# Block-diagonal 128x128 tiles for the inverted chunk matrices of a delta-rule recurrence

## The chip, the core and the metric

The kernel runs on one core of a Trainium2 chip. The metric is the device time of one execution in microseconds. Each time shown is the median of several executions. One further execution is recorded by the hardware profiler, and the rows below come from that one.

Names of engines: PE is the matrix engine, and PEld its loading of weights, which can run beside the products. DVE is the vector engine, ACT the scalar engine, POOL the third elementwise engine, and SP issues most of the DMAs.

## What is computed

One layer of a hybrid decoder over 1024 tokens of width 1024, in float32. A normalised input goes through one combined projection, then through two branches: sliding-window attention and an RWKV-7 recurrence with 8 heads of size 64. The branches are gated and merged, and a squared-ReLU MLP follows. The recurrence is what matters here:

```python
def step(S, inp):
    r_t, w_t, k_t, v_t, a_t, b_t = inp
    sa = jnp.einsum('bhij,bhj->bhi', S, a_t)
    S = S * w_t[:, :, None, :] + sa[..., None] * b_t[:, :, None, :] + v_t[..., None] * k_t[:, :, None, :]
    return S, jnp.einsum('bhij,bhj->bhi', S, r_t)
```

## The kernel before

**The recurrence in chunks.** The 1024 steps are cut into 16 chunks of 64 tokens. Heads go in pairs, so that a pair fills 128 partitions. A unit is one pair over one half of the sequence, that is 8 chunks. There are 8 units, run one after the other. For each unit `unit_e` prepares decays, keys and receptances. `unit_m` inverts a 64x64 triangular matrix for each chunk and head. `unit_c` carries the state from chunk to chunk.

**Where the inverses lie.** `unit_m` leaves the inverses, transposed, in the tile XT of shape 128x8x64. Even chunks of the unit stand on partitions 0 to 63 and odd chunks on 64 to 127. The middle index counts chunk pair and head. The inverse is finished by two ACT copies of 32x256 elements (line 619).

**The chain of one chunk** (`unit_c`) has these steps, each of which needs the one before it:

1. `ry` (line 636, PE): the old state times keys and receptances, one 128x128 product.
2. `G` (line 638, DVE): adds half of `ry` to the right-hand side `Rs`, a slice of the tile G0.
3. `pu` (lines 641 to 642, issued at line 162, PE): the inverse times `Rs`, one 64x64 product for each of two heads.
4. `UV` (line 643, DVE): copies `pu` out.
5. `pd` (line 646, PE): the update of the state, one 128x128 product.
6. `sbd` (lines 653 and 656, DVE): two operations that write the new state, which the next `ry` needs.

The weights of a float32 product are loaded twice and its columns run twice, so each of `ry` and `pd` has 2 PE rows in the trace, and `pu`, with its two heads, has 4.

**The order of work.** A scheduler lays down one fixed order for each engine when the kernel is built. The recurrence has a raised priority. Between its steps the scheduler puts "fill": products of the projections and gates (`ps_m`, line 156, 128x128 weights and 512 columns), attention (`ps_t`, `pt_t`, `po`) and low-rank projections (`ps_l`). A list of steps, PLAN, says which fill is on offer beside which unit. After the last unit the rest of the fill runs, then the branch projections, the output projection and the MLP. PE runs its rows strictly in the order laid down.

**Shapes of the array.** A PE row of the trace shows which part of the array a product uses: 128\*128 is all of it, 64\*64 a quarter, and 64\*128, 128\*64 and 32\*32 occur as well. The fill is 128\*128 almost everywhere. `pu` is 64\*64, and so are `ps_g`, `ps_z` and `ps_x` of `unit_m`. The readout `py` at the end of a unit is 128\*64.

Of the kernel before, what the change touches and what calls it, by code (L numbers as in the profile page):

```python
# [11 lines left out]
F32 = mybir.dt.float32  # L12
# [8 lines left out]
P = 128  # L21
# [37 lines left out]
def hybrid_block(ctx, tc, x_ap, xt_ap, win_ap, lora_ap, wbr_ap, wout_ap, wff1_ap, wff2_ap, cst_ap,  # L59
                 vec_ap, eye_ap, amk_ap, out_ap, dbg=None):  # L60
    nc = tc.nc
    V, A, G, PE = nc.vector, nc.scalar, nc.gpsimd, nc.tensor
# [28 lines left out]
    def c_(name):  # L91
        o, n = COFF[name]
        return cst[0][:, o:o + n] if o < CKEEP else cst[1][:, o - CKEEP:o - CKEEP + n]
# [65 lines left out]
    def in_order(mms, after=None):  # L159
        for out, lhsT, rhs, start, stop in mms:  # L160
            with tc.issue_after(after) if after is not None else nullcontext():
                after = PE.matmul(out=out, lhsT=lhsT, rhs=rhs, start=start, stop=stop).ins  # L162
        return after
# [77 lines left out]
    def phase1():  # L241
        st = ExitStack()
        lp = st.enter_context(tc.tile_pool(name="lpool", bufs=1))
        rp = st.enter_context(tc.tile_pool(name="rpool", bufs=1))
# [203 lines left out]
                    nc.sync.dma_start(out=g_d[p][:, sl], in_=t)  # L448

        sbd = [lp.tile([P, 128], F32, name=f"sbd{i}") for i in range(2)]  # L450
        for t in sbd:
            G.memset(t, 0.0)
        ln_d = [dram.tile([64, 256], F32, name=f"ln_d{i}") for i in range(8)]
        lx_d = [dram.tile([P, 128], F32, name=f"lx_d{i}") for i in range(8)]
# [115 lines left out]
        def unit_m(p, hf, X):  # L570
            SA, UV, un = X["SA"], X["UV"], X["un"]
            G0 = rp.tile([P, 4, 128], F32, tag="G0", name="G0", bufs=1)
            half_ = [slice(0, 64), slice(64, 128)]
            ps = pp.tile([P, 4, 2, 64], F32, tag="c", name="ps_g", bufs=1)
            for i in range(4):
                for h in range(2):
                    for par in range(2):
                        uc, vc = half_[par], half_[1 - par]
                        PE.matmul(out=ps[uc, i, h], lhsT=SA[vc, par, 2 * i + h, :],
                                  rhs=UV[vc, 2 * i + par, h * 64:h * 64 + 64], start=True, stop=True)  # L580
            A.copy(out=G0, in_=ps.rearrange("p a b c -> p a (b c)"))
            XT = rp.tile([P, 8, 64], F32, tag="XT", name="XT", bufs=2)
            G.memset(XT, 0.0)
            lx = lx_d[un].rearrange("(q l b u) (c t) -> q b (u c) l t", l=8, b=2, u=2, t=16)
            for q in range(4):
                for b in range(2):
                    o = 32 * (q % 2) + 16 * b
                    s0 = 32 * q + 16 * b
                    nc.sync.dma_start(out=XT[s0:s0 + 16, :, o:o + 16], in_=lx[q, b])
            XD = rp.tile([P, 8, 64], F32, tag="DZ", name="XD", bufs=1)  # L590
            V.transpose(out=XD.rearrange("p a b -> p (a b)"), in_=XT.rearrange("p a b -> p (a b)"))
            ps = pp.tile([P, 8, 64], F32, tag="c", name="ps_z", bufs=1)
            for l in range(8):
                for par, uc in enumerate(half_):
                    PE.matmul(out=ps[uc, l], lhsT=SA[uc, par, l], rhs=XD[uc, l], start=True, stop=True)
            V.tensor_mul(out=XD, in0=ps, in1=c_("m16").unsqueeze(1).broadcast_to([P, 8, 64]))
            ps = pp.tile([P, 8, 64], F32, tag="c", name="ps_x", bufs=1)
            for l in range(8):
                for uc in half_:
                    PE.matmul(out=ps[uc, l], lhsT=XD[uc, l], rhs=XT[uc, l], start=True, stop=True)  # L600
            V.tensor_add(out=XT, in0=XT, in1=ps)
            DZ = rp.tile([P, 2, 8, 32], F32, tag="DZ", name="DZ", bufs=1)
            DT, Z = DZ[:, 0], DZ[:, 1]
            tops = [slice(64 * par, 64 * par + 32) for par in range(2)]
            lows = [slice(64 * par + 32, 64 * par + 64) for par in range(2)]
            for ta in tops:
                V.transpose(out=DT[ta], in_=XT[ta, :, 0:32])
            ps = pp.tile([P, 8, 32], F32, tag="c", name="ps_z", bufs=1)
            for l in range(8):
                for par, (ta, lb) in enumerate(zip(tops, lows)):  # L610
                    PE.matmul(out=ps[lb, l], lhsT=SA[ta, par, l, 32:64], rhs=DT[ta, l], start=True, stop=True)
            for lb in lows:
                A.copy(out=Z[lb], in_=ps[lb])
            ps = pp.tile([P, 8, 32], F32, tag="c", name="ps_x", bufs=1)
            for l in range(8):
                for ta, lb in zip(tops, lows):
                    PE.matmul(out=ps[ta, l], lhsT=Z[lb, l], rhs=XT[lb, l, 32:64], start=True, stop=True)
            for ta in tops:
                A.copy(out=XT[ta, :, 32:64], in_=ps[ta])
            X.update(G0=G0, XT=XT)  # L620

        def unit_c(p, hf, X):
            us = slice(hf * HALF, (hf + 1) * HALF)
            ARf, UV, BKt, SR, bv, wc, G0, XT = (X[n] for n in ("ARf", "UV", "BKt", "SR", "bv", "wc", "G0", "XT"))
            Yt = rp.tile([P, 4, 2, 64], F32, tag="Yt", name="Yt", bufs=2)
            for c in range(8):
                par, cp = c % 2, c // 2
                first = hf == 0 and c == 0
                uc, vc = slice(64 * par, 64 * par + 64), slice(64 - 64 * par, 128 - 64 * par)
                cur, nxt = sbd[par], sbd[1 - par]  # L630
                ry = pp.tile([P, 2, 64], F32, tag="r", name="ry", bufs=1)
                Rs = G0[:, cp, :]
                if first:
                    G.memset(Yt[vc, cp], 0.0)
                else:
                    PE.matmul(out=ry.rearrange("p a b -> p (a b)"), lhsT=ARf[:, cp, par], rhs=cur, start=True,
                              stop=True)
                    V.tensor_add(out=Rs[uc], in0=Rs[uc], in1=ry[uc].rearrange("p a b -> p (a b)"))
                    A.copy(out=Yt[vc, cp], in_=ry[vc])
                pu = pp.tile([P, 128], F32, tag="c", name="pu", bufs=1)  # L640
                last = in_order([(pu[uc, h * 64:h * 64 + 64], XT[uc, 2 * cp + h], Rs[uc, h * 64:h * 64 + 64], True,
                                  True) for h in range(2)])
                V.tensor_copy(out=UV[uc, c, :], in_=pu[uc])
                if hf == 0 or c < 7:
                    pd = pp.tile([P, 128], F32, tag="c", name="pd", bufs=1)
                    PE.matmul(out=pd, lhsT=BKt[:, c], rhs=UV[:, c], start=True, stop=True)
                    if not first:
                        sw = rp.tile([P, 128], F32, tag="sw", name="sw", bufs=2)
                        A.activation(out=sw, in_=cur, func=AF.Copy, scale=wc[:, c:c + 1])
                    for h in range(2):  # L650
                        hs = slice(h * 64, h * 64 + 64)
                        if first:
                            V.tensor_scalar(out=nxt[hs, hs], in0=pd[hs, hs], scalar1=wc[hs, c:c + 1],
                                            scalar2=None, op0=ALU.mult)
                        else:
                            V.scalar_tensor_tensor(out=nxt[hs, hs], in0=pd[hs, hs], scalar=wc[hs, c:c + 1],
                                                   in1=sw[hs, hs], op0=ALU.mult, op1=ALU.add)
# [73 lines left out]
        for n in range(8):  # L731
            p, hf = n // 2, n % 2
            with tc.high_priority(offset=HP_C):
                unit_m(p, hf, xs[n])
            if hf == 0 and p + 1 < NPAIR:
                zproj(p + 1)
            if n + 1 < 8:
                estage(n + 1)
            with tc.high_priority(offset=HP_C):
                unit_c(p, hf, xs[n])  # L740
            fill(PLAN[n + 1])
        st.close()

    def gate(i):
        w = load_w(win_ap[20 + i])
        for hf in range(2):
# [3 lines left out]
            nc.sync.dma_start(out=gate_d[i][:, hf * HALF:(hf + 1) * HALF], in_=t)  # L750

    phase1()
    bst = ExitStack()
    bp = bst.enter_context(tc.tile_pool(name="bpool", bufs=1))
    yh = [bp.tile([P, T], F32R, name=f"yh{k}") for k in range(8)]
    yl = [bp.tile([P, T], F32R, name=f"yl{k}") for k in range(8)]
    for k in range(8):
        t = bp.tile([P, T], F32, tag="yt", name="yt", bufs=3)
# [35 lines left out]
    h = [hall[:, k] for k in range(NK)]  # L794
# [404 lines left out]
```

## Time and profile before

| what | value |
|---|---|
| time, median of 3 runs | 1538.51 us (1537.07 to 1538.57) |
| profiled execution, its own time | 1539.05 us |
| its span, first to last instruction | 1537.3 us |
| mean granted TensorE clock | 0.999 |
| PE busy | 1491.2 us, 97% of the span |
| DVE busy | 1039.3 us, 68% |
| ACT busy | 638.9 us, 42% |
| POOL busy | 195.3 us, 13% |

The span leaves out 1.75 us of the execution's own time. Busy time is a sum over instructions. Products are pipelined and their recorded ends are modelled, so what one product costs is read from the distance between starts, not from its duration.

### The profile page before, as it was taken

How to read it: one execution, taken by the hardware profiler on the slowest of the kernel's cores; microseconds unless marked ns; L12 is line 12 of the kernel's file. 1: busy time of each engine (PE TensorE's matmuls, PEld its weight loads, DVE VectorE, ACT ScalarE, POOL GpSimd, SP SyncE). 2: the span in 40 equal slices, each digit the busy share in tenths (PEclk: the TensorE clock that was granted, in tenths of full speed). 3: DMA queues.
4: the chain of work that ended last, by engine and by line, in shares of the span. 5: the costliest groups of instructions: out<-in, count | busy, mean ns of one | idle time of the engine just before them, and what ended most of it. 6: DMA issues, size and time to landing. Idle time of an engine off the chain costs nothing.

```text
span 1537.3 us, 22192 instructions
## 1 busy us (share of the span) xinstructions
PE 1491.2 (97%) x8396; PEld 1179.0 (77%) x8396; DVE 1039.3 (68%) x2055; ACT 638.9 (42%) x1126; POOL 195.3 (13%) x117
## 2 busy tenths in 40 slices
PE   5999999999999999999999989999999999999998
PEld 5877767777777777788878777878787878787776
DVE  4232678888989875344656569495968587776767
ACT  6322446556545655532224343242334243424332
POOL 1000000000000000000000112322323232323230
PEclk9999999999999999999999999999999999999999
DMA  5455334334322324372442111112011111111112
GB/s 191 164 154 139 109 117 133 111 97 118 97 83 65 99 97 140 126 268 103 157 152 89 41 41 49 62 41 69 31 66 41 69 42 55 55 54 43 55 55 110
DMA packets 99771, 145.65 MB, mean 95 GB/s; under 512 B 26448, under 2 KB 48848, under 8 KB 99664
## 3 DMA queue, kind: packets, MB, share of 16 engines
q1 hardware_dynamic: 99664, 144.23, 28.6%
q8 instruction: 66, 1.08, 0.3%
q14 instruction: 41, 0.34, 0.1%
HBM read 108.54 MB, written 35.65 MB: 94 GB/s over the span
## 4 chain that ended last, share of the span: by engine, by line
PE 76%; DVE 18%; issue 2%; DMA 2%; ACT 1%; SPq 0%; DVEq 0%; ACTq 0%
PE ps_m L156 31%; PE psy L982 17%; PE psx L982 12%; DVE wlo L924 2%; PE po L156 2%; PE ps_o L915 1%; PE pu L162 1%; DVE h L1082 1%; DVE c L987 1%; DVE tlo L1010 1%; DVE c L1057 1%; DVE c L1015 1%; DVE c L1017 1%; PE pk L238 1%; PE ps_s L162 1%
## 5 line engine op out<-in xcount | busy, mean ns | idle before, releaser
L156 PE MATMUL ps_m<-uh,wlo 128*128 128x512 f32 x576 | 235.4, 409 | 0.0
L156 PE MATMUL ps_m<-ul,whi 128*128 128x512 f32 x576 | 234.3, 407 | 0.0
L156 PE MATMUL ps_m<-uh,whi 128*128 128x512 f32 x576 | 232.9, 404 | 0.0
L982 PE MATMUL psy<-T,whi 128*128 128x512 f32 x512 | 159.6, 393 | 0.0
L156 PEld LDWEIGHTS ps_m<-uh,wlo 128*128 128x128 f32 x576 | 108.6, 189 | 21.2 <-issue 0.6
L156 PEld LDWEIGHTS ps_m<-uh,whi 128*128 128x128 f32 x576 | 108.6, 189 | 21.1 <-issue 0.8
L156 PEld LDWEIGHTS ps_m<-ul,whi 128*128 128x128 f32 x576 | 108.7, 189 | 20.1 <-issue 0.7
L982 PEld LDWEIGHTS psy<-T,whi 128*128 128x128 f32 x512 | 96.1, 188 | 21.6
L982 PE MATMUL psx<-tlo,whi 128*128 128x512 f32 x256 | 101.9, 398 | 7.3 <-DVE tlo L1010 7.3
L982 PE MATMUL psy<-T,wlo 128*128 128x512 f32 x256 | 101.4, 396 | 4.4 <-DVE wlo L924 4.4
L149 DVE TENSOR_TENSOR wlo<-wraw,whi 128x512 fp32r<-128x512 f32 x101 | 67.8, 687 | 55.9 <-ACT whi L148 55.8
L924 DVE TENSOR_TENSOR wlo<-fraw,whi 128x1024 fp32r<-128x1024 f32 x47 | 62.3, 1326 | 62.8 <-ACT whi L923 62.8
L982 PE MATMUL psx<-thi,wlo 128*128 128x512 f32 x256 | 101.1, 396 | 0.9 <-DVE h L1082 0.9
L982 PE MATMUL psx<-thi,whi 128*128 128x512 f32 x256 | 101.1, 395 | 0.0
L1082 DVE TENSOR_TENSOR h<-h,psx 128x1024 f32<-128x1024 f32 (+1 forms) x66 | 78.0, 1183 | 20.3 <-PE psx L982 20.0
L953 POOL TENSOR_TENSOR fraw<-fraw,fraw 128x1024 f32<-128x1024 f32 x16 | 43.0, 2686 | 348.4 <-DVE s L929 347.3
L923 ACT CAST whi<-fraw 128x1024 fp32r<-128x1024 f32 x47 | 49.2, 1046 | 82.3 <-PE psx L982 57.3
L1010 DVE TENSOR_TENSOR tlo<-c,thi 128x1024 fp32r<-128x1024 f32 x56 | 78.2, 1397 | 2.2 <-ACT thi L1009 2.2
L148 ACT CAST whi<-wraw 128x512 fp32r<-128x512 f32 x105 | 61.0, 619 | 44.2 <-PE ps_m L156 44.1
L982 PE MATMUL psy<-thi,wlo 128*128 128x512 f32 x192 | 75.8, 395 | 0.0
L982 PE MATMUL psy<-thi,whi 128*128 128x512 f32 x192 | 75.7, 395 | 0.0
L982 PE MATMUL psy<-tlo,whi 128*128 128x512 f32 x192 | 75.7, 394 | 0.0
(300 smaller groups left out, 3230.5 us busy)
## 6 DMA issues: line engine op xcount, KB each, us to landing
wraw<-win SPq DMA_DIRECT2D x72, 256.0 KB, 3.3
fraw<-wff SPq DMA_DIRECT2D x32, 512.0 KB, 3.2
wraw<-wff SPq DMA_DIRECT2D x32, 512.0 KB, 3.2
gate_d<-gt SPq DMA_DIRECT2D x32, 256.0 KB, 2.0
z_d<-zt SPq DMA_DIRECT2D x24, 256.0 KB, 2.1
xt<-x SPq DMA_DIRECT2D x8, 512.0 KB, 5.7
la<-wa_d SPq DMA_DIRECT2D x8, 512.0 KB, 4.3
aq<-q_d SPq DMA_DIRECT2D x8, 512.0 KB, 4.4
```

Of the source, the lines that this page charges most:

```text
L148: A.copy(out=hi[:, ks], in_=raw[:, ks])
L149: (eng or V).tensor_sub(out=lo[:, ks], in0=raw[:, ks], in1=hi[:, ks].bitcast(F32))
L156: PE.matmul(out=out, lhsT=a, rhs=b, start=(n == 0), stop=(n == last))
L162: after = PE.matmul(out=out, lhsT=lhsT, rhs=rhs, start=start, stop=stop).ins
L238: PE.matmul(out=ps_out[:, col + 2 * i:col + 2 * i + 2], lhsT=sq[:, i * 128:(i + 1) * 128], rhs=c_("ind"), start=True, stop=True)
L915: PE.matmul(out=pss[j], lhsT=a, rhs=b[:, sl], start=(k == 0 and n == 0), stop=(k == NK - 1 and n == 2))
L923: A.copy(out=hi, in_=src)
L924: V.tensor_sub(out=lo, in0=src, in1=hi.bitcast(F32))
L953: G.tensor_sub(out=a21, in0=a11, in1=a21)
L982: PE.matmul(out=out, lhsT=a, rhs=b, start=start and n == 0, stop=n == last, skip_group_check=True)
L1010: V.tensor_sub(out=lo, in0=src, in1=hi.bitcast(F32))
L1082: V.tensor_add(out=ht, in0=ht, in1=ps[:, c0 % 2:c0 % 2 + step])
```

## The change

`unit_m` copies each finished inverse into a tile XB of shape 128x8x128. Even chunks go to its upper left 64x64 block and odd chunks to its lower right one. Two such tiles, `xbd`, are set to zero once, and units take them in turn. The products `pu` then use all 128 partitions and 128 weight columns. The copy out still takes the 64 partitions of the chunk at hand. XT itself has one buffer in place of two.

```diff
         sbd = [lp.tile([P, 128], F32, name=f"sbd{i}") for i in range(2)]
-        for t in sbd:
+        xbd = [lp.tile([P, 8, 128], F32, name=f"xbd{i}") for i in range(2)]
+        for t in sbd + xbd:
             G.memset(t, 0.0)
...
-            XT = rp.tile([P, 8, 64], F32, tag="XT", name="XT", bufs=2)
+            XT = rp.tile([P, 8, 64], F32, tag="XT", name="XT", bufs=1)
             G.memset(XT, 0.0)
...
                 A.copy(out=XT[ta, :, 32:64], in_=ps[ta])
-            X.update(G0=G0, XT=XT)
+            XB = xbd[un % 2]
+            for uc in half_:
+                A.copy(out=XB[uc, :, uc], in_=XT[uc])
+            X.update(G0=G0, XT=XB)
...
-                last = in_order([(pu[uc, h * 64:h * 64 + 64], XT[uc, 2 * cp + h], Rs[uc, h * 64:h * 64 + 64], True,
-                                  True) for h in range(2)])
+                last = in_order([(pu[:, h * 64:h * 64 + 64], XT[:, 2 * cp + h], Rs[:, h * 64:h * 64 + 64], True, True)
+                                 for h in range(2)])
                 V.tensor_copy(out=UV[uc, c, :], in_=pu[uc])
```

Lines behind the first edit stand one further down in the changed kernel, and lines in `unit_c` four further down: `ry` is line 640 there, and `pd` line 650. The scheduler's order changes with the edits. On PE the two orders agree up to the first `pu` and again from 641.7 us of the trace before on.

On PE, from the last products of the first unit's inverse (`ps_x`) to the `pu` of its second chunk, there stood before:

```order
L617 MATMUL ps_x<-XT,DZ 32x32 x16
L156 MATMUL ps_m<-uh_143,whi 128x512
L156 MATMUL ps_m<-uh_144,wlo 128x512
L156 MATMUL ps_m<-ul_152,whi 128x512
L156 MATMUL ps_m<-uh_144,whi 128x512
L162 MATMUL pu<-G_1447,XT 64x64 x2
L156 MATMUL ps_m<-uh_145,wlo 128x512
L156 MATMUL ps_m<-ul_153,whi 128x512
L156 MATMUL ps_m<-uh_145,whi 128x512
L646 MATMUL pd<-UV,BKt 128x128
```

At the same place on PE there stands now:

```order
L156 MATMUL ps_m<-uh_145,whi 128x512
L343 MATMUL ps_t<-ak,aq 128x128
L162 MATMUL pu<-G_1451,xbd_480 128x64 x2
L344 MATMUL ps_t<-ak,aq 128x128
L343 MATMUL ps_t<-ak,aq 128x128
L344 MATMUL ps_t<-ak,aq 128x128
L650 MATMUL pd<-UV,BKt 128x128
L640 MATMUL ry<-sbd_479,AR 128x128
L162 MATMUL pu<-G_1451,xbd_480 128x64 x2
```

Eight pieces of fill now stand ahead of the first `pu`, where four did. Behind it `pd`, `ry` and the second `pu` follow each other with nothing between.

On ACT, in the first unit, what follows the two copies that finish the inverse was before:

```order
L619 COPY XT<-ps_x 32x8x32 x2
L438 ACTIVATE lt<-lt 128x512
L195 COPY zt<-ps_m 128x512
L442 CAST gh__2167<-lt 128x512
L649 ACTIVATE sw<-sbd_479,wc 128x128
```

At the same place on ACT there stands now:

```order
L620 COPY XT<-ps_x 32x8x32 x2
L623 COPY xbd_480<-XT 64x8x64 x2
L195 COPY zt<-ps_m 128x512
L438 ACTIVATE lt<-lt 128x512
L148 CAST whi<-wraw 128x512 x2
```

The two copies into the block-diagonal tile come directly behind, in every unit. The copy of a projection out of its accumulator (`zt`) now stands behind them.

On PE, in the unit that uses `G_3636`, at its last chunks there stands now:

```order
L162 MATMUL pu<-G_3636,xbd_481 128x64 x2
L156 MATMUL ps_m<-ul_151,whi 128x512
L156 MATMUL ps_m<-uh_143,whi 128x512
L156 MATMUL ps_m<-uh_144,wlo 128x512
L650 MATMUL pd<-UV,BKt 128x128
L156 MATMUL ps_m<-ul_152,whi 128x512
L156 MATMUL ps_m<-uh_144,whi 128x512
L156 MATMUL ps_m<-uh_145,wlo 128x512
L156 MATMUL ps_m<-ul_153,whi 128x512
L156 MATMUL ps_m<-uh_145,whi 128x512
L640 MATMUL ry<-sbd_479,AR 128x128
L162 MATMUL pu<-G_3636,xbd_481 128x64 x2
```

Here too `pu` follows `ry` directly. The usual piece of fill, three products of 512 columns between `pu` and `pd`, stands as it did before.

## Rows read from the trace of the kernel before

**Rows 1.** Busy time by stage: start and end, length, busy us (x instructions) per engine.

```profile
core 0: us, PE busy (x) PEld busy (x) DVE busy (x) ACT busy (x) POOL busy (x), PEclk, DMA share, GB/s
219.40:575.40 356.00, 352.27 (x3157) 265.47 (x3158) 305.86 (x1092) 206.97 (x515) 5.88 (x28) 1.00 0.33 102
...
641.70:1537.30 895.60, 872.51 (x3754) 702.26 (x3752) 602.66 (x576) 306.09 (x355) 181.06 (x63) 1.00 0.23 78
```

**Rows 2.** Instructions on the tile pu: counts, ns min/median/max, first and last start.

```profile
L162 PE MATMUL pu<-G,XT x256: 218/218/267, 219.4 to 575.2; 64*64 64x64 f32 x128
L643 DVE COPY UV<-pu x64: 255/289/297, 219.9 to 575.4; 64x128 f32<-64x128 f32 x64
```

**Rows 3.** Timeline of one chunk in the first unit: start, duration, engine, line, what.

```profile
229.22 0.46 PE L636 MATMUL ry<-sbd,AR 128*128 128x128 f32 x2
...
229.85 0.29 DVE L638 TENSOR_TENSOR G<-G,ry 64x128 f32<-64x128 f32 x1
229.98 0.40 PE L156 MATMUL ps_m<-ul,whi 128*128 128x512 f32 x1
...
230.31 0.30 PEld L162 LDWEIGHTS pu<-G,XT 64*64 64x64 f32 x4 [0.36 <-DVE G L638]
...
230.68 0.50 PE L156 MATMUL ps_m<-uh,whi 128*128 128x512 f32 x1
...
230.85 0.29 DVE L643 COPY UV<-pu 64x128 f32<-64x128 f32 x1
...
231.02 0.39 PE L156 MATMUL ps_m<-uh,wlo 128*128 128x512 f32 x1
...
231.25 0.39 PE L156 MATMUL ps_m<-ul,whi 128*128 128x512 f32 x1
231.25 0.42 PEld L646 LDWEIGHTS pd<-UV,BKt 128*128 128x128 f32 x2
...
231.48 0.38 PE L646 MATMUL pd<-UV,BKt 128*128 128x128 f32 x2
...
231.62 0.48 PE L156 MATMUL ps_m<-uh,whi 128*128 128x512 f32 x1
...
231.93 0.27 PE L380 MATMUL pt_t<-cst,sm 128*128 128x128 f32 x1
...
232.24 0.58 DVE L656 SCALAR_TENSOR_TENSOR sbd<-pd,wc,sw 64x64 f32<-64x64 f32 x2
...
232.87 0.49 PE L636 MATMUL ry<-sbd,AR 128*128 128x128 f32 x2
...
233.12 0.48 PE L156 MATMUL ps_m<-uh,wlo 128*128 128x512 f32 x1
...
233.43 0.39 PE L156 MATMUL ps_m<-ul,whi 128*128 128x512 f32 x1
```

**Rows 4.** Timeline of PE at 247.8 us: eight products with two columns each.

```profile
247.82 1.05 PE L238 MATMUL pk<-cst,sq 128*128 128x2 f32 x8
248.74 0.42 PE L380 MATMUL pt_t<-cst,sm 128*128 128x128 f32 x2
```

**Rows 5.** Waits of the weight loads, 219.4 to 575.4 us: us in total, times, longest.

```profile
PEld pu L162 <- DVE G L638: 11.6, 31, 0.7
PEld pd L646 <- DVE UV L643: 1.7, 6, 0.4
```

**Rows 6.** Timeline from the end of the first unit's inverse to its first pu.

```profile
217.68 0.69 PE L617 MATMUL ps_x<-XT,DZ 32*32 32x32 f32 x32
...
218.42 0.74 ACT L619 COPY XT<-ps_x 32x256 f32<-32x256 f32 x2 [0.27 <-PE ps_x L617]
```

**Rows 7.** Instructions on the tile UV: the nearest ACT copy, 64x512.

```profile
L560 ACT COPY UV<-pt x8: 577/578/579, 180.5 to 506.5; 64x512 f32<-64x512 f32 x8
```

**Rows 8.** Timeline of POOL where the zeroing stands.

```profile
38.28 0.53 POOL L583 MEMSET XT<- 128x512 f32 x1
...
41.15 0.10 POOL L406 MEMSET z<- 128x1 f32 x1 [1.55 <-DVE lt L414]
```

## The prediction

> **What bounds the kernel now.** I read the stages first. From the first `pu` to the last, 219.4 to 575.4 us, PE is busy for 352.3 of 356.0 us, DVE for 305.9 (86%) and ACT for 207.0 (58%) [rows 1]. So PE's work sets the time there, and DVE has little to spare. The orders of PE agree again from 641.7 us on, so the 895.6 us behind that [rows 1] are no subject here. Then I read one chunk on the timeline, since the question is what one `pu` costs PE and what else hangs on it.
>
> A piece of fill starts every 0.23 us in the dense stream (231.02, 231.25) [rows 3]. From the fill at 229.98 to the second fill behind `pu` at 231.02 are 1.04 us; two of them account for 0.47, so the group of four 64\*64 products costs **0.57 us**. Likewise `pd`: from 231.25 to the second product behind it at 231.93 are 0.68, less 0.46 makes **0.22 us** for two loads of 128 columns [rows 3]. In the stage's 22 clean cases of `pu` between fills, the median is 0.57; in 12 of `pd` it is 0.22. A small product is set by its loads: eight with only two columns take 0.92 us, 0.115 each [rows 4].
>
> So the small array costs more than its loads. A new `pu` group has four full-width loads, twice those of `pd`: **0.44 us**, whatever its 64 columns.
>
> By the Trainium skill, page "TensorEngine Tiling (Array Packing)", section "Key Properties", a change of tiling mode, not only of tile, drains the engine; the row agrees, since 0.57 us is more than the loads explain. By the Trainium skill, page "TensorE: Matmul & The Clock Gate", section "LDWEIGHTS (loading the stationary operand)", a load takes its columns over 1.2 GHz, which speaks against the change: an estimate from it is 0.053 us more per load, 0.21 per group. By the first rule alone a group would fall to its old loads, by the second alone it would rise to 0.78; the rows give 0.44, since both act.
>
> **Term 1, PE's work.** There are 64 groups (256 rows) [rows 2]. In the order of before, 52 have full-array work on both sides. Each saves 0.13: -6.8 us. Eight run on into `py`, which keeps its own shape: one of two changes stays, at about 0.1, and the loads grow by 0.2. I put +0.1 each: +0.8. Four stand beside 64\*128 work and still change shape twice: +0.2 each, +0.8. In the new order shape changes fall from 324 to 217, where swapping `pu` in the old order would leave 212. The five extra ones, at about 0.1 each, make +0.6. Sum: **-4.6 us**.
>
> **Term 2, the hand-overs to DVE.** This is where I expect the saving to go. The drain around `pu` was idle time of PE, and the chain used it. In the shown chunk `G` ends at 230.14 [rows 3]. The load of `pu` is released about 0.05 later, 230.19. With no drain PE wants that load 0.11 before the fill from 229.98 has run through (230.21), at 230.10. It comes late, and a late load loses its cover: `ry`, released late at 232.87, has its second fill at 233.43 [rows 3]. That is 0.33 for two products, three loads in a row, where the dense `pd` paid two. So the new `pu` gives PE back at 230.19 + 5 x 0.11 = 230.73, against 231.02 - 0.23 = 230.79 now. It gains 0.06 in place of 0.13.
>
> Its last product also starts later behind the load: four full loads, 0.43, against 0.18 now. Its record lasts 0.22 [rows 2], and `UV` starts 0.04 behind it at the earliest: 0.26. `UV` would end at 230.19 + 0.43 + 0.26 + 0.29 = 231.17 and release `pd` at 231.22. PE, back early, wants it at 231.25 - 0.06 = 231.19. So 0.03 more goes, and 0.03 us of 0.13 is left in this chunk.
>
> I did this sum for the 56 groups that follow full-array work, from the rows of the timeline for `G`, `pu`, `UV` and `pd` (64 copies `UV`, first at 219.9, last at 575.4) [rows 2]. In 18 `G` is early enough for a covered load, in 10 partly, in 28 the load is late. The views of waits say the same: `G` released 31 loads of `pu`, 11.6 us in all, and `UV` only 6 of `pd`, 1.7 us [rows 5]. Summed, 7.2 us of a saving of about 7.3 go back. The new order has slightly more fill between `ry` and `pu`, and three groups belong to term 3, so I take **+6.0 us**. The bounds are 0, if DVE is always in time, and 64 x 0.25 = 16, if the longer path sets every chunk.
>
> **Term 3, places without cover.** In the first chunk `ps_t` products cover `pu` to `pd` for 0.35, where about 0.6 is needed. Then `pd`, `ry` and `pu` follow each other directly. From `pd` at 231.48 to a release of `ry` are 0.38 for its record, 0.1, two `sbd` of together 0.58 and 0.05, less its own slot 0.22: 0.9 idle. From `ry` at 229.22 to the end of `G` at 230.14 are 0.92, less 0.22: 0.7 [rows 3]. The unit of `G_3636` has one more such place, 0.7. Sum 0.25 + 0.9 + 0.7 + 0.7: **+2.5 us**. Below, it is 0 if PE is late there anyway; above, 4 if DVE has other work queued.
>
> **Term 4, the copies and the zeroing.** No row shows a copy of 64x512 between two such tiles; the nearest, from an accumulator, takes 0.58 [rows 7]. Two per unit make 1.16 us on ACT, on the way from inverse to first `pu`; over 8 units 9.3. ACT has room, but its queue holds the release of accumulators (`zt`) and the scaled states (`sw`) behind them, for which PE and DVE wait. The way now needs 0.26 to the first copy, 0.74 for the old pair [rows 6], 1.16 and 0.05: 2.2 us. The new order puts 1.8 to 3.3 us of PE work there (before 1.0 to 2.1). Three units fall short by 0.2 to 0.4, others nowhere: **+0.5 us**, between 0 and 9.3. Zeroing `xbd` costs POOL two operations of twice a 0.53 us one; next in its queue, `z` at 41.15 waits for DVE anyway [rows 8]. Early in the kernel that is worth 0. One XT buffer is also worth 0: the next unit's zeroing needs only the copies, which precede the first `pu`.
>
> **Sum.** -4.6 + 6.0 + 2.5 + 0.5 = +4.4 us. On the profiled execution's 1539.05 us (span 1537.3 and 1.75 around it) this is 1543.4. That execution is 0.54 above the median, so the time is 1538.5 + 4.4 = **1542.9 us**. A difference under 0.2%, 3.1 us, can't be told from none.
>
> **The rivals.**
> - *The saving is kept (faster).* The scheduler's fill covers the path and DVE is early. For it speaks that waits in this stage are small now, PE being busy 99% of it [rows 1]. Against it, 28 late loads. It decides at term 2: below about 1.5 us, with term 3 near 0 because PE arrives late, the kernel is faster. Time 1538.5 - 4.6 = 1533.9, by term 1 alone. The page on tiling, by its drain rule (the Trainium skill), points this way.
> - *Give-back and saving cancel (same).* DVE's other work moves with PE, so some late loads turn early and the bare places cost half. Term 2 at 3.5, term 3 at 1.1, term 4 at 0: 1538.5. For it: the shown chunk keeps a little.
> - *The recurrence becomes the bound (slower still).* If path and DVE queue exceed PE's work in most chunks, term 2 is 16: -4.6 + 16 + 2.5 + 0.5 = +14.4, or 1552.9. Against it: 18 groups have their `G` early.
> - *Nothing is undone.* If the price came from the size of the copy or the columns and not from the change of shape, four wider loads would add to 0.57 and the time would rise by 64 x 0.2 = 13, to 1551. Against it: `pd` and `ry`, with the same fill around them, pay no such extra.
>
> **Chances.** Forecast 0.37, from +3.1 to +9 us (1541.6 to 1547.5). Same 0.34 (1535.4 to 1541.6). Faster 0.22 (down to 1532). The two slower rivals 0.07 together. Slower is thus 0.44. The range runs from 1533.5 to 1548, leaving out the lower end of the faster case and the two slower rivals.
>
> **What the new profile would show.** Term 1: between fills the group `pu` at 128\*128 costs 0.43 to 0.45 where its load was in time. Term 2: loads of `pu` released by `G` and of `pd` released by `UV` wait in more cases than 31 and 6, and late groups cost about 0.55. Term 3: PE gaps of 0.5 to 1 us at the first chunk. Term 4: pairs of copies of about 0.58 us ahead of each unit's first `pu`. Behind 641.7 us of before, the stages should be equally long. I am wrong if the stretch from the first `pu` to that point (422.3 us before) is shorter by more than 3 us, or if time moves behind it.

## The result: 1.4% slower, and the profile after

The changed kernel takes **1560.06 us** (median of 4 runs, 1558.0 to 1562.85), where the kernel before took 1538.36 beside it. The ratio is 1.0144 [1.0125, 1.0163]. The forecast was 1542.9 in a range from 1533.5 to 1548: the direction was right, the size far off. The profiled execution is the quickest of the four, so the trace accounts for 18.9 us of the 21.7 between the medians.

| what | value after |
|---|---|
| profiled execution, its own time | 1558.0 us |
| its span | 1556.2 us |
| mean granted TensorE clock | 0.995 |
| PE busy | 1502.9 us, 97% |
| DVE busy | 1042.3 us, 67% |
| ACT busy | 648.5 us, 42% |

First the stages by the view of busy time, columns as in [rows 1].

```profile
220.20:588.20 368.00, 357.87 (x3121) 275.54 (x3121) 305.83 (x1080) 214.09 (x524) 6.52 (x30) 0.99 0.32 97
661.80:1556.20 894.40, 872.39 (x3753) 702.38 (x3751) 599.70 (x574) 303.90 (x352) 182.16 (x63) 1.00 0.21 74
```

Behind the recurrence nothing is lost: 894.4 us where there were 895.6 [rows 1]. From the first `pu` to the point where PE's orders agree again there are now 441.6 us (220.2 to 661.8) where there were 422.3. The first `pu` starts 0.8 later. Together +20.1, less 1.2 behind: the 18.9 us between the spans.

Where in that stretch? PE's order is known, and dense stretches of the trace before show what most kinds of row cost there, from start to start (a piece of fill 0.23; a wide `pu` group is put at twice a `pd`, 0.44). The sum over the rows of an order is **PE's work**. What a stretch takes beyond it is **lost**. Both are estimates, good to some 3 us in a sum over eight stretches. "Loops" are the eight stretches from a unit's first `pu` to the last row of its last one; "between" is the seven from there to the next first `pu`.

| kernel | time, us | ratio to before [interval] | loops: time | PE's work | lost | lost between |
|---|---|---|---|---|---|---|
| before | 1538.4 | | 213.0 | 209.4 | 3.6 | 1.3 |
| after | 1560.06 | 1.0144 [1.0125, 1.0163] | 215.0 | 197.0 | 18.0 | 10.3 |
| e1 wide, no copies | 1543.63 | 1.0029 [1.0019, 1.0039] | 215.9 | 204.5 | 11.5 | 1.0 |
| e2 copies, narrow | 1545.81 | 1.0041 [1.0027, 1.0054] | 213.6 | 209.8 | 3.8 | 1.7 |
| e3 early copies | 1548.55 | 1.0056 [1.0036, 1.0077] | 218.1 | 204.1 | 14.0 | 2.7 |
| e4 copies on POOL | 1548.89 | 1.0057 [1.0037, 1.0076] | 216.0 | 202.3 | 13.7 | 5.1 |
| e7 wide, one `sbd` | 1538.53 | 0.9996 [0.9987, 1.0006] | 194.8 | 188.3 | 6.5 | 1.9 |
| e9 before, one `sbd` | 1537.10 | 0.9992 [0.9983, 1.0001] | 198.2 | 197.1 | 1.2 | 1.2 |
| e8 after, priority | 1548.68 | 1.0059 [1.0044, 1.0074] | 213.2 | 197.9 | 15.3 | 5.6 |
| e11 before, priority | 1539.72 | 1.0009 [1.0000, 1.0018] | 211.1 | 208.4 | 2.7 | 4.4 |
| e10 split copies | 1548.81 | 1.0067 [1.0054, 1.0081] | 216.9 | 205.2 | 11.7 | 9.7 |
| e12 split, plan | 1544.24 | 1.0037 [1.0023, 1.0051] | 215.2 | 203.9 | 11.3 | 4.5 |

In after, PE's work up to that point fell by 5.4 us. The loops lose 14.4 more (3.4 of it in the first unit), the stretches between 9.0, the tail behind the last `pu` 1.2, and the start is 0.8 later. That is the +20.0.

**What a group costs.** Timeline of PE in after: start, duration, engine, line, what.

```profile
287.63 0.39 PE L156 MATMUL ps_m<-uh,wlo 128*128 128x512 f32 x1
287.86 0.55 PE L162 MATMUL pu<-G,xbd 128*128 128x64 f32 x4
288.22 0.48 PE L156 MATMUL ps_m<-ul,whi 128*128 128x512 f32 x1
288.54 0.40 PE L156 MATMUL ps_m<-uh,whi 128*128 128x512 f32 x1
```

From 287.63 to 288.54 are 0.91 us, less 0.47 for two pieces of fill: 0.44 for the group, where [rows 3] gave 0.57. Of the 20 groups that stand between fill, 7 cost at most 0.47 and 12 over 0.50; the median is 0.54. So the saving is there, but only where the load is in time. The median of those 12 is 0.65, more than the 0.57 of before.

**The first chunk.** Timeline of after.

```profile
220.22 0.63 PE L162 MATMUL pu<-G,xbd 128*128 128x64 f32 x4 [0.30 <-issue]
...
221.23 0.49 PE L650 MATMUL pd<-UV,BKt 128*128 128x128 f32 x2
...
222.52 0.49 PE L640 MATMUL ry<-sbd,AR 128*128 128x128 f32 x2 [0.81 <-DVE sbd L657]
...
223.50 0.66 PE L162 MATMUL pu<-G,xbd 128*128 128x64 f32 x4 [0.49 <-DVE G L642]
```

PE stands idle for 0.81 and 0.49 us, each time for the DVE result before.

**The end of the fourth unit.** Timeline of after, PE and DVE.

```profile
401.66 0.66 PE L162 MATMUL pu<-G,xbd 128*128 128x64 f32 x4 [0.76 <-DVE G L642]
...
402.25 1.20 PE L162 MATMUL py<-UV,SR 128*64 128x64 f32 x32
...
403.38 1.15 PE L580 MATMUL ps_g<-UV,SA 64*64 64x64 f32 x32
...
406.10 0.42 DVE L518 SCALAR_TENSOR_TENSOR BK<-kkn,Wi 128x256 f32<-128x256 f32 x1
406.17 1.16 PE L162 MATMUL ps_s<-AR,BK 64*128 64x128 f32 x16 [1.64 <-DVE BK L518]
406.44 0.68 DVE L675 TENSOR_TENSOR Yt<-Yt,mean 128x512 f32<-128x512 f32 x1
...
407.04 0.74 DVE L552 SCALAR_TENSOR_TENSOR r<-r,vec,k 128x512 f32<-128x512 f32 x1
...
407.88 0.69 DVE L679 TENSOR_REDUCE var<-ysq 128x8 f32<-128x512 f32 x1
...
408.48 0.41 DVE L529 TENSOR_TENSOR SA<-ps_s,cst 128x256 f32<-128x256 f32 x1
...
408.88 0.42 DVE L529 TENSOR_TENSOR SR<-ps_s,cst 128x256 f32<-128x256 f32 x1
...
409.45 2.85 PE L162 MATMUL ps_s<-AR,BK 64*128 64x128 f32 x16 [2.12 <-DVE nw L131]
...
409.69 0.42 DVE L529 TENSOR_TENSOR SR<-ps_s,cst 128x256 f32<-128x256 f32 x1
```

`ps_s` belongs to `unit_e` of a later unit. Its second 16 rows write into the two accumulators of the first 16. The first of these is free when `SA` and `SR` are copied out of it (L529), which stand on DVE behind `Yt`, `r` and `var`. That `SR`, from 408.88 on, ends at 409.30 and PE goes on at 409.45. The trace names `nw`, which ended later by 0.08; I take it for a bystander. PE has nothing to do meanwhile: in its order the second 16 rows follow the first directly. The three gaps make 0.76 + 1.64 + 2.12 = 4.5 us.

Then the granted clock, last figure but two of each row of the view of busy time in after:

```profile
219.50:225.10 5.60, 3.96 (x25) 3.06 (x23) 4.44 (x18) 4.03 (x8) 0.56 (x2) 1.00 0.30 107
225.10:228.50 3.40, 3.21 (x12) 2.54 (x10) 2.79 (x12) 1.47 (x3) 0.00 (x0) 0.50 0.25 96
...
401.00:409.40 8.40, 4.02 (x84) 3.56 (x84) 8.22 (x22) 4.21 (x9) 0.21 (x2) 1.00 0.28 76
409.40:416.20 6.80, 6.71 (x57) 5.91 (x58) 4.77 (x17) 0.00 (x0) 0.10 (x1) 0.50 0.35 64
```

Behind either place PE runs at half clock, 1.2 GHz: for 3.4 us after 5.6 in which it was busy for 3.96, and for 6.8 us after 8.4 in which it was busy for 4.02. Sixteen rows of `ps_s` then last 2.85 us, where they had lasted 1.16 at 406.17. Not all of that is the clock: the products go to the two accumulators in turn, and the second is free only when its `SR` from 409.69 ends at 410.11. In the kernel before, the stretch from 401.0 to 409.4 us looked like this:

```profile
401.00:409.40 8.40, 8.23 (x93) 6.40 (x94) 8.32 (x30) 3.50 (x7) 0.10 (x1) 1.00 0.34 83
```

DVE is just as full (8.32 against 8.22), but PE has fill beside it. In after the last piece of fill starts at 400.28, before the last `ry` of the unit.

### The profile page after: what moved, and what is told of

It reads as the page before. It is cut to its first block, busy times and chain, and to the rows that moved or that the text cites. A ratio compares the mean times of both kernels' runs of the same rounds, so it can differ in the third digit from the quotient of the medians.

```text
span 1556.2 us, 22228 instructions
## 1 busy us (share of the span) xinstructions
PE 1502.9 (97%) x8396; PEld 1194.0 (77%) x8396; DVE 1042.3 (67%) x2055; ACT 648.5 (42%) x1142; POOL 198.3 (13%) x119
## 4 chain that ended last, share of the span: by engine, by line
PE 75%; DVE 18%; issue 3%; ACT 2%; DMA 2%; SPq 0%; DVEq 0%; ACTq 0%
PE ps_m L156 31%; PE psy L986 17%; PE psx L986 11%; DVE wlo L928 2%; PE pu L162 2%; PE po L156 1%; PE ps_o L919 1%; DVE h L1086 1%; DVE c L991 1%; DVE tlo L1014 1%; DVE c L1061 1%; DVE c L1019 1%; DVE c L1021 1%; PE ry L640 1%; PE pk L238 1%
## 5 line engine op out<-in xcount | busy, mean ns | idle before, releaser
L156 PEld LDWEIGHTS ps_m<-uh,wlo 128*128 128x128 f32 x576 | 108.8, 189 | 20.1 <-issue 0.9
```

Of the source, the lines that this page charges most:

```text
L156: PE.matmul(out=out, lhsT=a, rhs=b, start=(n == 0), stop=(n == last))
```

## The experiments

The expectations name the theories by letters. **A**: PE loses the time in a few places without fill, where it idles and its clock then falls. **B**: the wide products lengthen the path from hand-over to hand-over and cost in every chunk. **C**: the copies themselves hold things up. **D**: a change of the array's shape costs PE, against **L** (loads alone) and **R** (rows used).

### e1: the wide products alone

```diff
-  in_order([(pu[uc, h*64:h*64+64], XT[uc, 2*cp+h], Rs[uc, ...
+  in_order([(pu[:, h*64:h*64+64], XT[:, 2*cp:2*cp+2, :].rearrange("p a b -> p (a b)"), Rs[:, ...
```

> The products pu are 128x128 with the same columns as after the change, but their weights are a slice of XT itself (both heads side by side, all partitions), so there are no copies, no zeroed tiles, and XT keeps two buffers. What this leaves out: the right inverse, so the state carries other values. In its order PE has no bare place in the recurrence (least work between two steps of the chain 0.5 us). Theory A (a few places without fill, where PE idles and its clock falls, make the loss): 1538.4 less 3.7 us of PE work, 1533 to 1538, and no half-clock stretch between 219 and 640 us. Theory B (the longer path through the wide products limits PE in every chunk, about 11 us over the units): 1543 to 1549, still without a half-clock stretch. Theory C (the copies on ACT make the loss): as A.

Measured: 1543.63 us, 5.1 above before and in B's range. There is no place like those above (1.0 us lost between units) and no half clock in the recurrence, yet the loops lose 11.5 us where before lost 3.6. PE's work is 3.7 us less. So B is a real cost, about 8 us (11.5 less 3.6), but e1 has only 5.1 of the changed kernel's 21.7 us.

### e2: the copies, the products narrow

```diff
-  ... (pu[:, h*64:h*64+64], XT[:, 2*cp+h], Rs[:, ...
+  ... (pu[uc, h*64:h*64+64], XT[uc, 2*cp+h, uc], Rs[uc, ...
```

> Copies, zeroed tiles and one XT buffer as after the change, but pu stays 64x64 and reads its block of the tile. Its order has three poorly covered steps (0.1, 0.1, 0.25 us) and 2.1 us more PE work than before. Theory A: the poorly covered steps cost 1 to 4 us, 1541 to 1546, more only where the clock falls. Theory B: the path per chunk is the old one, so 1540 to 1544. Theory C: most of the 22 us is here already, 1552 to 1560.

Measured: 1545.81 us, 7.2 above before. The loops lose 3.8, no more than before. In the profiled execution 5.3 us go elsewhere between first `pu` and 650 us: PE's work is 1.8 more, and the tail loses 2.8 more. There attention waits for a load from memory, and 3.4 us at half clock follow from 620.9. Timeline of PE in e2:

```profile
620.17 0.36 PE L343 MATMUL ps_t<-ak,aq 128*128 128x256 f32 x1 [1.85 <-DMA ak<-k_d]
```

In before this wait took 0.9 us, and the clock stayed; in after it took 1.9, in two parts. So in this trace the 7.2 us are not time that the chain of a chunk waits for copies; they go with the new order. The time is in A's range, above B's and far below C's.

### e3 and e4: the copies earlier, or on POOL

e3 copies before the inverse's last block is done and writes that block straight into `xbd`. e4 puts the copies on POOL:

```diff
-                A.copy(out=XB[uc, :, uc], in_=XT[uc])
+                G.tensor_copy(out=XB[uc, :, uc], in_=XT[uc])
```

> As after the change, but the two copies into the block-diagonal tile are made before the last block of the inverse is computed, and that block is copied straight into the tile, so that nothing is added between the last products of the inverse and the first pu. The result is the reference's. Its order has one step covered by 0.27 us only and no bare one; PE work is 2.6 us below before. Theory A: 1535 to 1540. Theory B: 1545 to 1550. Theory C (the copies cost wherever they stand, as ACT time): 1550 to 1558.

> As after the change, with the two copies per unit on POOL in place of ACT. PE's work and its number of shape changes are those after the change (217), but its order has no bare place (least cover 0.4 us) and no long stretch without fill at the end of the fourth unit. Theory A: 1533 to 1540, and no half-clock stretch in the recurrence. Theory B: 1545 to 1550. Theory C: 1533 to 1541, as ACT is relieved.

Measured: 1548.55 and 1548.89 us. Each takes some 11 us off the changed kernel, though ACT is relieved in one and not in the other. The copies are as many in both, but the order differs, and with it the place at the fourth unit is gone (1.0 and 0.9 us lost there, 7.9 in after; e3 has 3.4 us at half clock elsewhere, from 323.2). That fits A for this place better than C. The times say more: they lie in B's range (1545 to 1550) in both, above A's (up to 1540), and outside C's, below it in e3 and above it in e4. A alone is too little. The 14 us that the loops lose are those of B and 2 to 3 more.

### e5 and e6: which part of the array, which loads

Both keep an order of PE that is known: e5 that of before, e6 that of e1.

```diff
 e5  (pu[:, h*64:h*64+64], XT[:, 2*cp+h], Rs[:, ...          128 rows, 64 columns
 e6  (pu[:, ...], XT[uc, 2*cp:2*cp+2, :].rearrange(...), Rs[uc, ...   64 rows, 128 columns
```

> From the kernel before, with one thing changed: the weights of pu take all 128 rows but 64 columns, a slice of XT over all partitions (shape 128*64 of the array, not 64*64). The order of every engine is that of before, row for row. What this leaves out: the other chunk's rows are added in, so the values are other ones. If it is the change of array shape that costs (theory D), 128*64 is still not the fill's 128*128: a group stays at 0.57 us and the time at 1537 to 1540. If the number of rows used is what matters (theory R), the group falls to some 0.3 us and the time to 1525 to 1533.

> Weights of pu with 64 rows and 128 columns (shape 64*128): the full-width loads of the change, with the change of array shape kept. The order of every engine is that of the run with wide products alone (1543.6 us), row for row. Left out: the products of the two heads land side by side, so the values are other ones. Theory D: the drain comes back and the wide loads stay, about 0.2 us per group on PE over before and a longer path too: 1552 to 1562. If the change of shape costs nothing and the loads all (theory L): 1542 to 1545, as with wide products.

Measured: e5 1538.35 us, ratio 0.9993 [0.9984, 1.0002]; e6 1551.92, ratio 1.0081 [1.0064, 1.0098], just under D's range and far above L's. Timeline of PE in e5, then in e6:

```profile
269.86 0.39 PE L156 MATMUL ps_m<-uh,whi 128*128 128x512 f32 x1
270.17 0.45 PE L162 MATMUL pu<-G,XT 128*64 128x64 f32 x4
270.55 0.50 PE L156 MATMUL ps_m<-uh,wlo 128*128 128x512 f32 x1
270.88 0.40 PE L156 MATMUL ps_m<-ul,whi 128*128 128x512 f32 x1
```

```profile
231.83 0.40 PE L156 MATMUL ps_m<-uh,whi 128*128 128x512 f32 x1
232.16 0.66 PE L162 MATMUL pu<-G,XT 64*128 64x64 f32 x4
232.75 0.50 PE L156 MATMUL ps_m<-uh,wlo 128*128 128x512 f32 x1
233.09 0.39 PE L156 MATMUL ps_m<-ul,whi 128*128 128x512 f32 x1
```

e5: 1.02 - 0.47 = 0.55 (median of 22 cases 0.57), as 64\*64. R falls. e6: 1.26 - 0.47 = 0.79 (median of 26 cases 0.78, all 0.77 or more). Against 0.44 without a change of shape, the change into `pu` and out again costs 0.34. L falls, D holds. By the Trainium skill, page "TensorEngine Tiling (Array Packing)", section "Key Properties", a change of tiling mode drains the engine; e5 agrees, since filling all rows but not all columns saves nothing.

The pair says more. The orders of e1 and e6 are the same, and e6 has 324 changes of shape where e1 has 222. At 0.17 each, the 102 more are an estimated 17.3 us for PE. e6 takes 8.3 us longer. So e1 spends some 9 us waiting that e6 does not, about as much as its loops lose beyond before's (7.9): the drain is time in which DVE's hand-overs get done.

### e7 and e9: a shorter path from `pd` to `ry`

One 128x128 DVE operation for the new state, in e7 on e1, in e9 on before:

```diff
-  for h in range(2):
-      hs = slice(h * 64, h * 64 + 64)
-      ... V.scalar_tensor_tensor(out=nxt[hs, hs], in0=pd[hs, hs], ..., in1=sw[hs, hs], ...)
+  ... V.scalar_tensor_tensor(out=nxt, in0=pd, scalar=wc[:, c:c + 1], in1=sw, ...)
```

> The run with wide products alone, and the two DVE operations that write the new state (64x64 each) made one of 128x128: the path of a chunk is 0.29 us shorter and DVE has 17 us less to do. Left out: the blocks between heads of the state are not kept at zero. PE's work is 1.8 us less by its order. Theory B (the path through a chunk limits PE where pu is wide: 11.5 us of PE time in the units beyond its work, 3.6 before): that falls to 6 or less and the time to 1533 to 1538. If not the path but PE's own price of the wide products is undercounted: the 11.5 stay and the time is 1540 to 1543.

> The kernel before with one 128x128 DVE operation for the new state in place of the two of 64x64; the blocks between the two heads are then left in the state, so the values are wrong. It is the control of the run that did the same to the wide products and gained 5.1 us. Theory B, that the step from pd to ry costs PE only where the longer wide product has used up the fill: before lost only 3.6 us in its eight loops, so at most 3 can come back, and PE's work in the new order is 0.2 less: 1535.5 to 1538.5 us. Rival, that the gain had nothing to do with the wide product's path but comes from 17 us less DVE work and the other order: the same 5 us come off here too, 1532.5 to 1534.5.

Measured: e7 1538.53 us, 5.1 below e1; e9 1537.10, 1.2 below before, ratio 0.9992 [0.9983, 1.0001], which can't be told from none. So the shorter path is worth much more beside the wide products. The one operation takes 0.35 us where the pair took 0.58, so the path is 0.23 us shorter, not 0.29, and DVE is busy for 14.1 us less (1026.5 against 1040.6), not 17. Late loads of `pu`, us in total, times, longest, by the view of waits of e1, then of e7:

```profile
PEld pu L162 <- DVE G L638: 8.6, 29, 0.5
```

```profile
PEld pu L162 <- DVE G L638: 2.6, 11, 0.3
```

The loops lose 6.5 instead of 11.5, a little over the 6 that B had allowed, and e7's time is half a microsecond above B's range. Both are far from the other reading (11.5 and 1540 to 1543). That supports B, with one reservation: DVE has less work in both, and the scheduler lays out another order (PE's work in the loops is 188 us, not 204), so the two effects aren't apart. Even so, the wide products gain nothing over e9.

### e8 and e11: another priority

```diff
-HP_E = 3000
+HP_E = 2800
```

> The changed kernel with the priority of unit_e 2800 in place of 3000, nothing else. PE's work is 1.4 us less by its order. Its order keeps the bare first chunk of the first unit, but has no long stretch without fill at the end of the fourth unit. Theory A (that stretch costs about 7.6 us of the change): 1548 to 1554, with no half-clock stretch near 400 us. If the loss is spread over all chunks: 1557 to 1561.

> The kernel before with only the raised priority of unit_e lowered from 3000 to 2800; nothing of the computation changes. It is the control of the two runs that lower it in the kernel after. Theory A, that 2800 helps the kernel after by closing a place without fill that its own order opened: before has no such place, so within 2 us of before, 1536.5 to 1540.5 us (PE's work is 0.9 less). Rival, that 2800 is simply the better number whatever the change: some 10 us less, 1527 to 1531.

Measured: 11.4 us off the changed kernel, to 1548.68, and 1539.72 for before, 1.0009 [1.0000, 1.0018]. View of busy time of e8:

```profile
224.40:227.80 3.40, 3.40 (x12) 2.79 (x12) 2.78 (x10) 1.19 (x3) 0.00 (x0) 0.50 0.24 92
380.00:420.00 40.00, 39.27 (x312) 30.14 (x313) 36.97 (x136) 23.60 (x56) 0.54 (x5) 1.00 0.31 93
```

The place at the fourth unit is covered and its half clock gone; the first chunk's remains. 2800 is no better number as such. A holds for this place. The profiled executions of after and e8 differ by 10.5 us, and the order of e8 is another one throughout, so not every microsecond of it is the place's.

### e10 and e12: both places covered

e10 is e8 with one copy of each pair on DVE. e12 also offers one gate projection (`x`) earlier as fill.

```diff
-            for uc in half_:
-                A.copy(out=XB[uc, :, uc], in_=XT[uc])
+            for eng, uc in zip((A.copy, V.tensor_copy), half_):
+                eng(out=XB[uc, :, uc], in_=XT[uc])
...
-PLAN = ("k v q q q q", "g", "a", "a", "a a", "a x", "a x x", "a x x", "a x x x x x x x x x")
+PLAN = ("k v q q q q", "g", "a", "a", "a a", "a x x", "a x x", "a x x", "a x x x x x x x x")
```

> The kernel after with one of each unit's two copies on DVE beside the other on ACT, and the raised priority of unit_e lowered from 3000 to 2800; nothing of the computation changes. In PE's order no chain step is left without fill: pd to ry and ry to pu have at least 0.68 and 0.33 us of other work, where the kernel after had places with 0, and the longest stretch without fill is 2.8 us where it had 5.9 and 5.1. PE's work is 6.7 us below before. Theory A, that the kernel after lost in its places without fill, the half clock behind them included, and theory B, that the longer wide product costs some 8 us in the loops wherever it stands: without the places only B's part is left, -6.7 + 8 = +1.4, so 1538 to 1543 us and no stretch at half clock between 219 and 640 us. Rival C, that the copies themselves hold the chain up on ACT and DVE: 9 us or more above before, as with the priority alone, 1547 to 1550.

Measured: 1548.81 us, where I had expected 1538 to 1543. That is the range of rival C. The first chunk was indeed covered (the first unit loses 2.3 us, as in e1), but the place at the fourth unit was back: 6.0 us lost. Timeline of PE, then the view of busy time of e10:

```profile
403.54 2.86 PE L162 MATMUL ps_s<-AR,BK 64*128 64x128 f32 x16 [1.89 <-DVE nw L135]
```

```profile
403.60:410.40 6.80, 6.68 (x30) 5.28 (x31) 6.74 (x27) 2.26 (x5) 0.10 (x1) 0.50 0.19 23
```

I had judged the places by how long PE's order goes without fill. That is the wrong measure. Here PE goes from one group of `ps_s` straight to the next, and what counts is the DVE queue that must empty its accumulators.

> The previous kernel (copies on ACT and DVE, priority 2800) with one gate projection offered as fill beside the fifth unit and one less beside the last; nothing of the computation changes. The trace of the previous one showed that a place need not be long in PE's order to cost: between the two groups of ps_s at the end of the fourth unit stood 0.06 us of other work, as in the kernel after, while DVE had to empty the accumulator of the first group behind a full queue; PE waited 1.9 us there and then ran 6.8 us at half clock. Now 1.6 us of fill stand there, and at least 1.2 between the two groups of any unit; pd to ry and ry to pu keep 0.68 and 0.33. Theory A, this place: without it and the half clock behind it 5 to 6 us come off 1548.8, 1542 to 1544.5 us, and no stretch at half clock between 219 and 640 us. Theory B says that what is then left, some 4 to 5 us above before, is the longer path of the wide products, 11 to 14 us without work in the eight loops against 3.6. Rival C, that the copies hold the chain up on ACT and DVE: the place changes little, 1547 to 1550.

Measured: 1544.24 us, 1.0037 [1.0023, 1.0051], inside the expectation of A. Timeline of PE, then the view of busy time of e12:

```profile
399.94 1.16 PE L162 MATMUL ps_s<-AR,BK 64*128 64x128 f32 x16
401.03 0.50 PE L156 MATMUL ps_m<-uh,whi 128*128 128x512 f32 x1
...
402.30 0.40 PE L156 MATMUL ps_m<-ul,whi 128*128 128x512 f32 x1
403.25 0.46 PE L162 MATMUL ps_s<-AR,BK 64*128 64x128 f32 x2 [0.55 <-DVE nw L136]
```

```profile
219.50:225.10 5.60, 5.04 (x29) 3.99 (x29) 5.19 (x20) 3.77 (x9) 0.11 (x2) 1.00 0.40 138
225.10:228.50 3.40, 3.27 (x19) 2.30 (x19) 3.28 (x13) 2.79 (x8) 0.10 (x1) 1.00 0.62 224
401.00:409.40 8.40, 7.84 (x51) 5.74 (x49) 8.40 (x35) 2.74 (x6) 0.10 (x1) 1.00 0.23 52
```

Six pieces of fill between the two groups leave a wait of 0.55 us, and the clock stays at 1.00, here as in the rest of the recurrence. C falls as the main cause: the copies are all there, on the same engines as in e10. What is left is 5.1 us over before (1539.15 beside it), and the loops lose 11.3 us as in e1. That e1 is 5.1 us over before too is in part chance: between units e12 loses 3.5 us more, as e11 does with 2800 and no copy (4.4 against before's 1.3), and its PE has less work, by the estimate. No version here is faster than before clear of the noise.

## Why the direction was right and the size wrong

**What bounds the kernel.** Right: PE's work, with DVE close behind, and nothing behind the recurrence moves.

**Term 1, -4.6.** Right: by the whole order of after PE's work is 4.6 us less (the 5.4 above count from the first `pu`, ahead of which four pieces of fill more now stand). A group costs 0.44 where its load is in time, as foreseen. The parts were off: a change of shape costs 0.17, not 0.1 (0.34 for the two, e6), and five changes at 0.1 are 0.5, not 0.6. That they cancel in the sum is luck.

**Term 2, +6.0.** The mechanism is shown by e1 against e6 and supported by e7 and e9; the size was low by some 2 us. Measured alone in e1 it is 11.5 - 3.6 = 7.9, in e12 7.7. The 12 costlier groups cost 0.65 in the median, where I said about 0.55 for late ones; over all 20 it is 0.54. The count of waits was a poor sign: `UV` released 14 loads of `pd` where it had released 6, but `G` only 28 of `pu` where it had released 31 [rows 5]. View of waits of after, 219 to 600 us:

```profile
PEld pu L162 <- DVE G L642: 9.4, 28, 1.0
...
PEld pu L162 <- ACT xbd L623: 3.7, 7, 0.9
PEld pd L650 <- DVE UV L647: 3.6, 14, 0.5
```

**Term 3, places without cover, +2.5. This is the step that failed.** The gaps that it priced came nearly as priced: 0.81 and 0.49 at the first chunk for 0.9 and 0.7, and 0.76 for 0.7 at `G_3636`. What it left out are two things. Behind `G_3636`'s `pu`, and the `py` and `ps_g` that follow it, `ps_s` stands as twice 16 rows with nothing between, and DVE's queue is full; this row was in the order, but I had looked for bare places only among the steps of the chain. And at both places the clock halves behind the gaps. Measured, the first unit loses 3.4 us more than before and the place at the fourth unit about 9 (7.9 less before's 0.3 behind its last `pu`, and 2.9 less 0.0 in its loop, part of which is term 2): some 12 for 2.5, an estimate, with a little of term 2 in the first unit's share too. e8, with the second place closed, takes 11.4 off, and e12, with both closed, 15.8; their orders differ elsewhere too.

How much of that is clock? From 409.45 to 416.24 PE has 6.8 us at half clock. The gaps between units there (1.64 + 2.12) leave 7.9 - 3.8 = 4.1 for it and for small waits, the one for the second accumulator among them. At the first chunk 3.4 us at half clock can cost up to 1.7, by estimate.

**Term 4, copies, +0.5.** A copy takes 0.62 us, where I had estimated 0.58. View of the tile `xbd` of after, counts and ns min/median/max:

```profile
L623 ACT COPY xbd<-XT x16: 614/619/622, 218.9 to 562.5; 64x512 f32<-64x512 f32 x16
L453 POOL MEMSET xbd<- x2: 948/952/955, 38.6 to 39.5; 128x1024 f32 x2
```

On the chain that is small. Loads of `pu` wait 3.7 us for the copies (the view under term 2), where they had waited 2.1 for XT, and between units e2 loses 1.7 against 1.3. But e2 costs 7.2 us altogether, with an order that has more PE work and a longer wait for a load from memory. I had priced the copies' way and not the new order.

**The rivals.** "The recurrence becomes the bound" gave 1552.9 for a path that binds in every chunk. The time went beyond it, but by the places, not by the path. "Nothing is undone" falls with the groups at 0.44. "The saving is kept" and "cancel" fall with e1: without a place and without copies it is still 5.1 us slower.

**What stays open.** Term 2's loss was not split chunk by chunk between `G`, `UV` and `sbd`, and e7 changed the order as well as the path. A control of the new PLAN in the kernel before was not run. Of e2's excess the tail is traced to the wait for `ak` and the clock behind it; why the load of `ak` came later against PE's work, and the rest, are not. No run closes the place at the fourth unit and changes nothing else.

## What to carry to other kernels

An idle time that sits on a dependent chain, here the drain at a change of shape, is not free to be taken: before counting it as a gain, ask which hand-over it hides, since some 9 of 17 us came back as waits (e1 against e6). When an edit makes a scheduler lay down a new order, read the whole new order for two dependent groups with nothing between them, not only the steps that were edited, and judge a place by the queue of the engine that must release it. Add to each such gap what the clock costs behind it.

## What the hardware showed unexpectedly

Between pieces of 128\*128 fill, products with 128 rows and 64 columns of the array cost a group 0.57 us, the same as 64\*64, and 64\*128 costs 0.78; only the fill's own shape, the full array, came down to 0.44. The clock fell to half behind stretches in which PE was busy for 3.96 of 5.60 us and 4.02 of 8.40 us. One DVE operation on 128x128 takes 0.35 us (e7), two on 64x64 take 0.58 (after, 221.89 to 222.47 for the pair).
